# Where weights and activations stand in SBUF: one 64-byte offset moved from the weights to the activations

## The chip, the core and the metric

One Trainium2 chip, of which the kernel uses one core (8 are there). The metric is the device time of one execution in microseconds; what is compared is the median of several executions.

## What is computed

The reference runs two networks one after the other on 256 tokens of width 1,024, all in 32-bit floats. The first has two layers, each made of a gated feed-forward (2,816 hidden), a token-mixing part with three branches (RWKV-7, gated linear attention, gated delta rule), a second feed-forward and a projection with a gate. The second has one layer of attention over the tokens and 256 context tokens, a feed-forward over both streams, one HGRN2 layer and a last feed-forward. Cut to the pieces that hold nearly all the weights:

```python
def _swiglu(x, w1, w3, w2):
    return (jax.nn.silu(x @ w1) * (x @ w3)) @ w2

def token_mixing(x, w_in, ...):
    h = (x @ w_in).astype(jnp.float32)
    h_rw, h_gla, h_gdn, h_gate = _split(h, GROUP_SPLITS)
    ...
    proj = jnp.einsum('btnc,ncd->btnd', branches, w_branch)
    merged = jnp.sum(gates * proj, axis=2)
    return merged.astype(x.dtype) @ w_o
```

## The kernel before, in words

All large products are made in a split form: an operand is held as `hi`, rounded to the matmul's own 32-bit type, and `lo`, the rest, and a product is three matmuls, hi x hi, lo x hi and hi x lo. Weights come in units of 512 KB (128 partitions x 1,024 numbers). `unit` (line 70) calls `split` (line 74): SyncE's queue loads the unit into a buffer `wr`, ScalarE copies it into `wh` (line 81), VectorE subtracts into `wl` (line 82). There are four buffers each of `wr` and `wh` and three of `wl`; a unit takes the next of each in turn, so the same pair of `wh` and `wl` comes back every twelve units. Activations lie in SBUF as `xh` and `xl`, made once per stage.

Two kinds of stage use the units. In a feature-major stage (`fm`, lines 105 to 112) a block of 128 x 128 weights is the stationary operand and 256 columns of `xh` or `xl` stream past it; 24 matmuls (8 blocks, 3 products) fill one PSUM tile. The feed-forward `ffn2` calls it for two units and each stream in turn: unit A with the first stream, unit B with the first, then A and B with the second where there is one. Here the third product of the first pair of units is made in a pass of its own (line 112). In a token-major stage (`tm2`, lines 181 to 183) a block of `xh` or `xl` is stationary and 512 columns of weights stream past (256 at a stage's end). TensorE's program is in this order, and every matmul is preceded by the load of its own stationary operand.

The five feed-forward stages with one stream begin at 8.6, 629, 863, 1,497 and 2,632 us of the profiled execution (each 1,056 feature-major matmuls and then the token-major ones on the hidden values `hh` and `hl`), the one with two streams at 1,963 us (2,112). Between them lie token mixing (15 + 12 + 4 single units, cut up by the branches' own work, twice), attention, and HGRN2's gates (24 units).

What this change is about is where those tiles lie in a partition. A tile pool is placed behind the pool before it, in the order in which they are opened, and takes its tiles times its buffers. In bytes, before the change:

| tile | first buffer | next buffers |
|---|---|---|
| `wr` | 22,176 | 4,096 apart |
| `wh` | 38,560 | 4,224 apart (4) |
| `wl` | 55,456 | 4,224 apart (3) |
| `xh`, `xl` of the first stream | 68,128 and 76,320 | one each |
| `xh`, `xl` of the second stream | 109,216 and 117,408 | one each |
| `hh` of feed-forwards 1 and 3, of 2, of 4 | 109,120, 127,552, 156,320 | |
| `hh` of the second network | 129,696 (second stream 174,752) | |
| `bh` (branches) | 160,320 | |

A buffer of `wh` or `wl` has 32 numbers (128 bytes) more than a unit, and the unit lies in it at an offset `at` that depends on the use: 16 numbers (64 bytes) in feature-major stages (`FM_AT`), 8 numbers (32 bytes) for `bh` and for the hidden values of the first network (`HID_AT`), 0 for all else. Blocks within a unit and within an activation are 512 or 1,024 bytes apart, so they do not change an address modulo 256.

Of the kernel before, what the change touches and what calls it, by code (L numbers as in the profile page):

```python
# [10 lines left out]
F32 = mybir.dt.float32  # L11
F32R = mybir.dt.float32r
# [5 lines left out]
P = 128  # L18
# [4 lines left out]
KF = 22  # L23
# [6 lines left out]
PIECES = (slice(0, 256), slice(256, 1024))  # L30


ROOM, FM_AT, HID_AT = 32, 16, 8


class Core:


# [14 lines left out]
    def open(self, es):  # L53
        tc = self.tc
        E = es.enter_context
        self.const = E(tc.tile_pool(name="const", bufs=1))
        self.wr = E(tc.tile_pool(name="wr", bufs=WR))
        self.wh = E(tc.tile_pool(name="wh", bufs=4))
        self.wl = E(tc.tile_pool(name="wl", bufs=3))
        self.xp = E(tc.tile_pool(name="xp", bufs=1))  # L60
        self.sm = E(tc.tile_pool(name="sm", bufs=4))
        self.fr = None
        self.mhalf = self.const.tile([P, 16], F32, name="mhalf")
        self.nc.gpsimd.memset(self.mhalf, -0.5)
        self.fc = E(tc.tile_pool(name="fc", bufs=1))
        self.mx = None
        self.dr = E(tc.tile_pool(name="dr", bufs=1, space=bass.MemoryType.DRAM))

    def unit(self, src, at=0):
        self.tick()
        return self.split(src, at)

    def split(self, src, at):
        nc = self.nc
        hi = self.wh.tile([P, 1024 + ROOM], F32R, tag="wh", name=self.nm("wh"))[:, at:at + 1024]
        lo = self.wl.tile([P, 1024 + ROOM], F32R, tag="wl", name=self.nm("wl"))[:, at:at + 1024]
        raw = self.wr.tile([P, 1024], F32, tag="wr", name=self.nm("wr"))
        nc.sync.dma_start(raw, src)  # L80
        on_act = nc.scalar.copy(hi, raw)  # L81
        on_dve = nc.vector.tensor_tensor(lo, raw, hi.bitcast(F32), ALU.subtract)  # L82
        if self.queue:
            for op, first in zip((on_act, on_dve), self.queue.pop(0)):
                self.behind(op, first)
        return hi, lo
# [48 lines left out]
    def ffn2(self, up, down, xs, scale, sink, aside={}):  # L135


        nc = self.nc
        with self.tc.tile_pool(name=self.nm("hp"), bufs=1, reuse_waits="tile") as hp:
            hs = []  # L140
            for i in range(len(xs)):
                hs.append((hp.tile([P, KF, T], F32R, tag=f"hh{i}", name=self.nm("hh")),
                           hp.tile([P, KF, T], F32R, tag=f"hl{i}", name=self.nm("hl"))))
            for m in range(KF):
                if m == 3:
                    self.load_later()
                if m in aside:
                    aside[m]()
                w = [self.unit(up[2 * m], FM_AT), self.unit(up[2 * m + 1], FM_AT)]
                for (xh, xl), (hh, hl) in zip(xs, hs):  # L150
                    pa, pv = self.acc(), self.acc()
                    self.fm([pa[:, :T], pv[:, :T]], w, xh, xl, late=m == 0)
                    th = hp.tile([P, T], F32, tag="th", bufs=3, name=self.nm("th"))
                    nc.scalar.activation(th, pa[:, :T], AF.Tanh, scale=0.5)  # L154
                    g = hp.tile([P, T], F32, tag="g", bufs=3, name=self.nm("g"))
                    nc.vector.scalar_tensor_tensor(g, th, 1.0, pa[:, :T], ALU.add, ALU.mult)
                    nc.vector.scalar_tensor_tensor(g, g, 0.5 * scale, pv[:, :T], ALU.mult, ALU.mult)  # L157
                    nc.scalar.copy(hh[:, m], g)  # L158
                    nc.vector.tensor_tensor(hl[:, m], g, hh[:, m].bitcast(F32), ALU.subtract)
            self.spot("down")  # L160
            self.tm2(down, 0, 2, hs, KF, sink, cut=True, at=0 if self.fr is None else HID_AT)

    def tm(self, src, b0, nblk, xh, xl, nk, sink, last=6, cut=False, at=0):
        self.tm2(src, b0, nblk, [(xh, xl)], nk, lambda n, i, t, ps, *c: sink(n, t, ps, *c), last, cut=cut, at=at)

    def tm2(self, src, b0, nblk, xs, nk, sink, last=6, lead=0, cut=False, at=0):

        nc = self.nc  # L170
        w = {}

        def mm(z, k, b, first, end):
            u = b // 2
            if u not in w:
                w[u] = self.unit(src[u], at)
            o, i, t, c = z
            h, l = (x[:, (b % 2) * 512 + c.start:(b % 2) * 512 + c.stop] for x in w[u])
            s = slice(t * P, t * P + P)
            xh, xl = xs[i]  # L180
            nc.tensor.matmul(o, xh[:, k, s], h, start=first, stop=False)  # L181
            nc.tensor.matmul(o, xh[:, k, s], l, start=False, stop=False)  # L182
            nc.tensor.matmul(o, xl[:, k, s], h, start=False, stop=end)  # L183

        self.load_later()
        for n in range(nblk):
            it = [(self.acc(), i, t, slice(0, 512)) for i in range(len(xs)) for t in range(2)]
            if cut and n == nblk - 1:
                o, i, t, _ = it.pop()
                it += [(o[:, :256], i, t, slice(0, 256)), (self.spare()[:, :256], i, t, slice(256, 512))]  # L190
            ahead = lead if n == 0 else 0
            tail = 0 if n < nblk - 1 else min(nk - ahead, last if len(xs) == 1 else last // 2)
            seq = [(k, z) for i in (1, 0) for k in range(ahead) for z in it if z[1] == i]
            seq += [(k, z) for k in range(ahead, nk - tail) for z in it]
            for k, z in seq:
                mm(z, k, b0 + n * nk + k, k == 0, k == nk - 1)
            for z in it:
                for k in range(nk - tail, nk):
                    mm(z, k, b0 + n * nk + k, k == 0, k == nk - 1)
                o, i, t, c = z  # L200
                sink(n, i, t, o, *((c,) if cut else ()))
# [884 lines left out]
class Block(Mix):  # L1086
# [15 lines left out]
    def proj(self, l, n, o):  # L1102

        nc = self.nc
        first = not self.merged
        bh = self.t([P, 4, T], "bh", F32R, pool=self.late)
        bl = self.t([P, 4, T], "bl", F32R, pool=self.late)
        self.to_fm(lambda t: o[:, t], bh, bl, nk=4)

        def sink(half, t, ps):  # L1110
            g = self.gt[n, half]
            nc.vector.scalar_tensor_tensor(g[:, t], g[:, t], 1.0, ps, ALU.add, ALU.mult)
            if first:
                self.merged[half] = g
            else:
                m = self.merged[half]
                nc.gpsimd.tensor_tensor(m[:, t], m[:, t], g[:, t], ALU.add)
        self.tm(self.a["wbr"][l, n], 0, 2, bh, bl, 4, sink, at=HID_AT)

    def rw_tile(self, i, ps, st={}):  # L1120
        nc = self.nc
# [21 lines left out]

    def fm_tile(self, i):
        p = self.acc()[:, :T]
        self.fm([p], [self.unit(self.wfm[i], FM_AT)], self.xh, self.xl)
        return p

    def token_mix(self, l, pool, ln):
# [121 lines left out]
    def first(self, es, ep, stop=None):  # L1271
        nc, tc, a = self.nc, self.tc, self.a
# [6 lines left out]

        def last_pool():  # L1280
            self.xq = es.enter_context(tc.tile_pool(name="xq", bufs=1, reuse_waits="tile"))
            self.xq.tile([P, 24], F32, name="fillq")
            return self.xq
        self.consts()
        self.x_load(pool())
# [46 lines left out]
class Second(Block):  # L1332
# [371 lines left out]
    def hgrn(self, h, st, xs):  # L1704
        nc, tc, a = self.nc, self.tc, self.a
        V = nc.vector
        with tc.tile_pool(name="hg", bufs=1, reuse_waits="tile") as p:
# [9 lines left out]
            m = tl([P, KD], "lm")  # L1717
# [17 lines left out]
            xh, xl = (self.xp.tile([P, KD, T], F32R, tag=f"x{c}0", name=self.nm("xo")) for c in "hl")  # L1735
# [5 lines left out]
            def gates(j):  # L1741
# [1 line left out]

                z = tl([P, 4, T], "z", bufs=2)
                for d in range(2):
                    w = self.unit(a["whfm"][3 * j + d], FM_AT)
                    ps = self.acc()
                    for i in range(2):
                        self.fm([ps[:, i * T:i * T + T]], [w], *xs[i])
                    nc.scalar.activation(z[:, d:4:2], ps.rearrange("p (i t) -> p i t", i=2), AF.Tanh, scale=0.5)  # L1750
                pq = self.acc()[:, :T]
                self.fm([pq], [self.unit(a["whfm"][3 * j + 2], FM_AT)], *xs[0])
# [5 lines left out]
                c, cx = tl([P, 4 * W], "c", bufs=2), tl([P, 2, W], "cx", bufs=2)  # L1758
# [134 lines left out]
            last = self.fetches([tl([P, 2, D], k) for k in ("qx", "kx", "v0", "v1")])  # L1893
# [204 lines left out]
```

## Time and profile before

| | us |
|---|---|
| runs of the kernel before | 2,810.91, 2,817.24, 2,833.98 |
| their median | 2,817.24 |
| the profiled execution, its own time | 2,826.01 |
| its span, first to last instruction | 2,824.2 |
| busy in the span: TensorE, VectorE, ScalarE, GpSimd | 2,723.2, 1,891.3, 1,299.3, 201.6 |

Every number from the trace belongs to the one profiled execution. The mean granted TensorE clock over the span is 0.983 of full speed. Busy time of TensorE counts a matmul from its issue to its modelled end, and matmuls overlap in the pipeline, so the mean of one matmul is longer than the time from its start to the next one's.

### The profile page before, as it was taken

To read this page: it belongs to the slowest core of one execution; us is meant where nothing else is said; L and a number is where in the kernel's file an instruction comes from. 1 tells how busy PE (TensorE), PEld (TensorE's weight loads), DVE (VectorE), ACT (ScalarE), POOL (GpSimd) and SP (SyncE) were. 2 spreads that over 40 slices of the span, in tenths; PEclk is the share of its full clock that TensorE was granted. 3 is DMA by queue.
4 is the path that set the end of the run, shared out by engine and by line. 5 is a ranking of instruction groups with operands and counts; after the bars stand their busy time and mean duration, and the time that the engine had idled before them with its cause. 6 is when DMAs were issued, how large, how long until landed. Compare 5 with 4: busy or idle time off the path is not lost.

```text
span 2824.2 us, 47580 instructions
## 1 busy us (share of the span) xinstructions
PE 2723.2 (96%) x18676; PEld 2403.6 (85%) x18676; DVE 1891.3 (67%) x3852; ACT 1299.3 (46%) x2040; POOL 201.6 (7%) x332
## 2 busy tenths in 40 slices
PE   9999999999999999999999998999999999999998
PEld 8978877669978978887778986798999888898897
DVE  6658885876557658876777756776444327799765
ACT  5536543535444536533444533564333225565553
POOL 0000211020000000211010001200000001000000
PEclk9999999999999999999999999999999999999999
DMA  7664333466666655323366556202332333214664
GB/s 257 195 207 162 113 123 111 143 235 194 195 225 205 194 181 181 120 95 117 120 219 233 187 172 226 83 10 89 105 98 90 127 102 110 75 57 145 196 194 152
DMA packets 117008, 426.63 MB, mean 151 GB/s; under 512 B 13600, under 2 KB 14112, under 8 KB 115760
## 3 DMA queue, kind: packets, MB, share of 16 engines
q1 hardware_dynamic: 115168, 419.01, 44.7%
q0 software_dynamic: 1472, 4.51, 0.5%
q8 instruction: 147, 2.41, 0.4%
q14 instruction: 77, 0.63, 0.1%
q10 hardware_dynamic: 144, 0.07, 0.0%
HBM read 420.36 MB, written 3.18 MB: 150 GB/s over the span
## 4 chain that ended last, share of the span: by engine, by line
PE 82%; DVE 11%; ACT 3%; DMA 2%; issue 2%; POOL 0%; DVEq 0%; POOLq 0%; SPq 0%; ACTq 0%
PE ps L105 12%; PE ps L106 12%; PE ps L108 12%; PE ps L182 10%; PE ps L181 10%; PE ps L183 10%; DVE wl L82 2%; PE pc L490 2%; PE pc L1653 1%; PE pc L1399 1%; PE pt L246 1%; PE pt L1637 1%; ACT wh L81 1%; PE pt L1840 1%; PE pc L661 1%
## 5 line engine op out<-in xcount | busy, mean ns | idle before, releaser
L82 DVE TENSOR_TENSOR wl<-wr,wh 128x1024 fp32r<-128x1024 f32 x658 | 813.1, 1238 | 524.0 <-issue 184.3
L81 ACT CAST wh<-wr 128x1024 fp32r<-128x1024 f32 x658 | 687.9, 1048 | 632.0 <-PE ps L183 294.2
L105 PE MATMUL ps<-xh,wh 128*128 128x256 f32 x3280 | 924.1, 283 | 11.7 <-ACT xh L250 5.9
L106 PE MATMUL ps<-xh,wl 128*128 128x256 f32 x3280 | 918.3, 281 | 3.3 <-DVE wl L82 3.3
L108 PE MATMUL ps<-xl,wh 128*128 128x256 f32 x3168 | 885.4, 280 | 0.1
L105 PEld LDWEIGHTS ps<-xh,wh 128*128 128x128 f32 x3280 | 624.4, 190 | 23.7 <-ACT xh L250 7.1
L106 PEld LDWEIGHTS ps<-xh,wl 128*128 128x128 f32 x3280 | 623.1, 190 | 9.6 <-DVE wl L82 4.4
L108 PEld LDWEIGHTS ps<-xl,wh 128*128 128x128 f32 x3168 | 598.5, 189 | 5.2 <-issue 4.1
L181 PE MATMUL ps<-wh,xh 128*128 128x512 f32 (+1 forms) x624 | 246.7, 398 | 5.2 <-ACT wh L81 3.0
L182 PE MATMUL ps<-wl,xh 128*128 128x512 f32 (+1 forms) x624 | 248.2, 398 | 0.8 <-DVE wl L82 0.8
L183 PE MATMUL ps<-wh,xl 128*128 128x512 f32 (+1 forms) x624 | 245.6, 395 | 0.0
L181 PE MATMUL ps<-wh,hh 128*128 128x512 f32 (+1 forms) x616 | 227.7, 370 | 0.1
L183 PE MATMUL ps<-wh,hl 128*128 128x512 f32 (+1 forms) x616 | 227.2, 369 | 0.0
L182 PE MATMUL ps<-wl,hh 128*128 128x512 f32 (+1 forms) x616 | 226.9, 368 | 0.0
L181 PEld LDWEIGHTS ps<-wh,xh 128*128 128x128 f32 x624 | 118.4, 190 | 36.6 <-ACT wh L81 3.5
L182 PEld LDWEIGHTS ps<-wl,xh 128*128 128x128 f32 x624 | 119.6, 192 | 26.1 <-DVE wl L82 2.1
L183 PEld LDWEIGHTS ps<-wh,xl 128*128 128x128 f32 x624 | 119.1, 191 | 23.8 <-issue 0.7
L181 PEld LDWEIGHTS ps<-wh,hh 128*128 128x128 f32 x616 | 115.7, 188 | 21.6 <-DVE g L157 0.5
L183 PEld LDWEIGHTS ps<-wh,hl 128*128 128x128 f32 x616 | 115.6, 188 | 21.1
L182 PEld LDWEIGHTS ps<-wl,hh 128*128 128x128 f32 x616 | 115.8, 188 | 20.7
L154 ACT ACTIVATE th<-ps 128x256 f32<-128x256 f32 x154 | 59.2, 385 | 151.9 <-PE ps L108 141.3
L158 ACT CAST hh<-g 128x256 fp32r<-128x256 f32 x154 | 62.6, 406 | 114.9 <-DVE g L157 114.8
(566 smaller groups left out, 3714.7 us busy)
## 6 DMA issues: line engine op xcount, KB each, us to landing
wr<-in_up SPq DMA_DIRECT2D x264, 512.0 KB, 4.2
wr<-in_down SPq DMA_DIRECT2D x132, 512.0 KB, 4.2
wr<-in_wtm SPq DMA_DIRECT2D x72, 512.0 KB, 3.3
wr<-in_wfm SPq DMA_DIRECT2D x62, 512.0 KB, 3.5
fr<-in_ada SPq DMA_DIRECT2D x23, 1024.0 KB, 5.8
wr<-in_ada SPq DMA_DIRECT2D x38, 512.0 KB, 4.3
wr<-in_wbr SPq DMA_DIRECT2D x24, 512.0 KB, 4.0
wr<-in_whfm SPq DMA_DIRECT2D x24, 512.0 KB, 3.3
```

The costliest lines, as they stand in the source:

```text
L81: on_act = nc.scalar.copy(hi, raw)
L82: on_dve = nc.vector.tensor_tensor(lo, raw, hi.bitcast(F32), ALU.subtract)
L105: nc.tensor.matmul(o, hi[:, w], xh[:, k], start=k == 0, stop=False)
L106: nc.tensor.matmul(o, lo[:, w], xh[:, k], start=False, stop=False)
L108: nc.tensor.matmul(o, hi[:, w], xl[:, k], start=False, stop=k == nk - 1)
L154: nc.scalar.activation(th, pa[:, :T], AF.Tanh, scale=0.5)
L158: nc.scalar.copy(hh[:, m], g)
L181: nc.tensor.matmul(o, xh[:, k, s], h, start=first, stop=False)
L182: nc.tensor.matmul(o, xh[:, k, s], l, start=False, stop=False)
L183: nc.tensor.matmul(o, xl[:, k, s], h, start=False, stop=end)
L246: nc.tensor.transpose(pt[:, j, t * P:t * P + P], self.cols(src(t), t, k + j), self.ident)
L490: nc.tensor.matmul(ps[:, 64 * u:64 * u + 64], lhs[:, u], rhs[:, u], start=True, stop=True)
```

## The change

The spare room in the weights' buffers goes, and with it the offsets of units: every unit starts at its buffer's edge and the buffers lie 4,096 bytes apart. Instead three unused tiles stand ahead of the activations: 64 bytes (`fillx`) ahead of `xh` and `xl` of the first stream, 32 bytes (`fillf`) in the pool behind, which moves all later pools, and in the last pool, which holds the second stream, 64 bytes in place of 96 (`fillq`). No instruction is added, taken away or reordered. The added line `raw = lo.bitcast(F32)` has no effect, as `raw` is set anew in the next line.

```diff
-ROOM, FM_AT, HID_AT = 32, 16, 8
...
         self.xp = E(tc.tile_pool(name="xp", bufs=1))
+        self.xp.tile([P, 16], F32, name="fillx")
...
         self.fc = E(tc.tile_pool(name="fc", bufs=1))
+        self.fc.tile([P, 8], F32, name="fillf")
...
-        hi = self.wh.tile([P, 1024 + ROOM], F32R, tag="wh", name=self.nm("wh"))[:, at:at + 1024]
-        lo = self.wl.tile([P, 1024 + ROOM], F32R, tag="wl", name=self.nm("wl"))[:, at:at + 1024]
+        hi = self.wh.tile([P, 1024], F32R, tag="wh", name=self.nm("wh"))
+        lo = self.wl.tile([P, 1024], F32R, tag="wl", name=self.nm("wl"))
+        raw = lo.bitcast(F32)
         raw = self.wr.tile([P, 1024], F32, tag="wr", name=self.nm("wr"))
...
-                w = [self.unit(up[2 * m], FM_AT), self.unit(up[2 * m + 1], FM_AT)]
+                w = [self.unit(up[2 * m]), self.unit(up[2 * m + 1])]
...
-            self.tm2(down, 0, 2, hs, KF, sink, cut=True, at=0 if self.fr is None else HID_AT)
+            self.tm2(down, 0, 2, hs, KF, sink, cut=True)
...
-            self.xq.tile([P, 24], F32, name="fillq")
+            self.xq.tile([P, 16], F32, name="fillq")
```

The rest of the diff takes `at` out of `unit`, `split`, `tm`, `tm2` and of their calls for the branches, the token mixing and the gates.

## Rows read from the trace of the kernel before

**Rows 1.** The page's head, busy time by engine, and the chain by engine.
```profile
span 2824.2 us, 47580 instructions
...
PE 2723.2 (96%) x18676; PEld 2403.6 (85%) x18676; DVE 1891.3 (67%) x3852; ACT 1299.3 (46%) x2040; POOL 201.6 (7%) x332
...
PE 82%; DVE 11%; ACT 3%; DMA 2%; issue 2%; POOL 0%; DVEq 0%; POOLq 0%; SPq 0%; ACTq 0%
```

**Rows 2.** The page's groups: count, busy us, mean ns, idle before.
```profile
L82 DVE TENSOR_TENSOR wl<-wr,wh 128x1024 fp32r<-128x1024 f32 x658 | 813.1, 1238 | 524.0 <-issue 184.3
```

**Rows 3.** Windows: us, busy PE, PEld, DVE, ACT, POOL (instructions), clock, DMA, GB/s.
```profile
20.00:130.00 110.00, 110.00 (x973) 110.00 (x972) 72.16 (x103) 56.79 (x84) 0.00 (x0) 1.00 0.66 212
...
1510.00:1620.00 110.00, 110.00 (x967) 110.00 (x967) 75.75 (x116) 58.83 (x87) 0.00 (x0) 1.00 0.57 190
...
1970.00:2210.00 240.00, 239.74 (x2060) 239.20 (x2059) 109.03 (x190) 81.07 (x138) 0.00 (x0) 1.00 0.30 97
```

**Rows 4.** Windows cut at the starts of groups of 24, two-stream feed-forward.
```profile
2051.76:2054.59 2.83, 2.83 (x26) 2.83 (x25) 0.85 (x2) 0.41 (x1) 0.00 (x0) 1.00 0.00 0
2054.59:2057.44 2.85, 2.85 (x26) 2.85 (x25) 1.56 (x2) 1.32 (x2) 0.00 (x0) 1.00 0.11 20
...
2065.82:2068.54 2.72, 2.72 (x27) 2.72 (x25) 1.55 (x2) 1.32 (x2) 0.00 (x0) 1.00 0.17 26
...
2085.20:2088.04 2.84, 2.84 (x26) 2.84 (x25) 0.84 (x2) 0.41 (x1) 0.00 (x0) 1.00 0.00 0
2088.06:2090.90 2.84, 2.84 (x26) 2.84 (x25) 1.56 (x2) 1.32 (x2) 0.00 (x0) 1.00 0.20 42
```

**Rows 5.** Windows of two groups of 24 in the last feed-forward.
```profile
2643.68:2646.51 2.83, 2.83 (x27) 2.83 (x25) 2.21 (x4) 1.62 (x4) 0.00 (x0) 1.00 0.64 217
2649.34:2652.06 2.72, 2.72 (x26) 2.72 (x26) 1.56 (x2) 1.32 (x2) 0.00 (x0) 1.00 0.54 176
```

**Rows 6.** Windows inside feature-major groups that follow a pause of TensorE.
```profile
205.55:207.67 2.12, 2.12 (x20) 2.12 (x19) 1.25 (x3) 1.53 (x2) 0.00 (x0) 1.00 1.04 425
1081.06:1083.66 2.60, 2.60 (x25) 2.60 (x24) 2.60 (x12) 1.93 (x3) 0.11 (x2) 1.00 0.00 0
2504.50:2506.86 2.36, 2.36 (x22) 2.36 (x21) 2.36 (x9) 1.73 (x3) 0.00 (x0) 1.00 0.00 0
```

**Rows 7.** Groups by shape, whole span: the first product of feature-major stages.
```profile
L105 PE MATMUL ps<-xh,wh 128*128 128x256 f32 x3280 | 924.1, 283 | 11.7 <-ACT xh L250 5.9 <-ACT wh L81 3.5 <-ACT xh L255 1.9
```

**Rows 8.** Groups by shape, 756 to 810 us: token-major, 512 and 256 columns.
```profile
L183 PE MATMUL ps<-wh,hl 128*128 128x512 f32 x62 | 24.4, 393 | 0.0
...
L181 PE MATMUL pc<-wh,hh 128*128 128x256 f32 x16 | 4.5, 281 | 0.0
```

**Rows 9.** Groups by shape, 30 to 130 us: feature-major, one stream.
```profile
L105 PE MATMUL ps<-xh,wh 128*128 128x256 f32 x295 | 81.4, 276 | 0.0
```

**Rows 10.** Groups by shape, whole span: one of three token-major products, 512 columns.
```profile
L182 PE MATMUL ps<-wl,xh 128*128 128x512 f32 x584 | 237.1, 406 | 0.8 <-DVE wl L82 0.8
...
L182 PE MATMUL ps<-wl,hh 128*128 128x512 f32 x484 | 190.0, 393 | 0.0
...
L182 PE MATMUL ps<-wl,xc 128*128 128x512 f32 x48 | 19.5, 407 | 2.3 <-DVE wl L82 2.3
...
L182 PE MATMUL ps<-wl,xo 128*128 128x512 f32 x24 | 9.7, 405 | 0.0
```

**Rows 11.** Window of 14 token-major matmuls of 512 columns, last feed-forward.
```profile
2783.18:2786.36 3.18, 3.18 (x16) 2.63 (x15) 2.11 (x3) 1.51 (x2) 0.00 (x0) 1.00 0.67 215
```

**Rows 12.** Windows of token-major stages: hidden values of feed-forwards 2, 4 and last.
```profile
756.00:810.00 54.00, 54.00 (x282) 45.97 (x281) 25.48 (x25) 19.94 (x19) 0.00 (x0) 1.00 0.59 193
1626.00:1682.00 56.00, 56.00 (x289) 47.37 (x288) 26.54 (x28) 20.38 (x20) 0.00 (x0) 1.00 0.58 188
2757.00:2812.00 55.00, 55.00 (x287) 47.01 (x286) 28.26 (x25) 20.70 (x23) 3.18 (x3) 1.00 0.50 163
```

More of the change, by code (lines that the diff above doesn't have):

```diff
@@ L65, in open, with unit, split @@
         self.fc = E(tc.tile_pool(name="fc", bufs=1))
+        self.fc.tile([P, 8], F32, name="fillf")
         self.mx = None
         self.dr = E(tc.tile_pool(name="dr", bufs=1, space=bass.MemoryType.DRAM))
-    def unit(self, src, at=0):
+    def unit(self, src):
         self.tick()
-        return self.split(src, at)
-    def split(self, src, at):
+        return self.split(src)
+    def split(self, src):
         nc = self.nc
-        hi = self.wh.tile([P, 1024 + ROOM], F32R, tag="wh", name=self.nm("wh"))[:, at:at + 1024]
-        lo = self.wl.tile([P, 1024 + ROOM], F32R, tag="wl", name=self.nm("wl"))[:, at:at + 1024]
+        hi = self.wh.tile([P, 1024], F32R, tag="wh", name=self.nm("wh"))
+        lo = self.wl.tile([P, 1024], F32R, tag="wl", name=self.nm("wl"))
+        raw = lo.bitcast(F32)
         raw = self.wr.tile([P, 1024], F32, tag="wr", name=self.nm("wr"))
@@ L160, in ffn2, with tm, tm2 @@
             self.spot("down")
-            self.tm2(down, 0, 2, hs, KF, sink, cut=True, at=0 if self.fr is None else HID_AT)
-    def tm(self, src, b0, nblk, xh, xl, nk, sink, last=6, cut=False, at=0):
-        self.tm2(src, b0, nblk, [(xh, xl)], nk, lambda n, i, t, ps, *c: sink(n, t, ps, *c), last, cut=cut, at=at)
-    def tm2(self, src, b0, nblk, xs, nk, sink, last=6, lead=0, cut=False, at=0):
+            self.tm2(down, 0, 2, hs, KF, sink, cut=True)
+    def tm(self, src, b0, nblk, xh, xl, nk, sink, last=6, cut=False):
+        self.tm2(src, b0, nblk, [(xh, xl)], nk, lambda n, i, t, ps, *c: sink(n, t, ps, *c), last, cut=cut)
+    def tm2(self, src, b0, nblk, xs, nk, sink, last=6, lead=0, cut=False):
         nc = self.nc
@@ L175, in mm @@
             if u not in w:
-                w[u] = self.unit(src[u], at)
+                w[u] = self.unit(src[u])
             o, i, t, c = z
@@ L1117, in sink @@
                 nc.gpsimd.tensor_tensor(m[:, t], m[:, t], g[:, t], ALU.add)
-        self.tm(self.a["wbr"][l, n], 0, 2, bh, bl, 4, sink, at=HID_AT)
+        self.tm(self.a["wbr"][l, n], 0, 2, bh, bl, 4, sink)
     def rw_tile(self, i, ps, st={}):
@@ L1145, in fm_tile @@
         p = self.acc()[:, :T]
-        self.fm([p], [self.unit(self.wfm[i], FM_AT)], self.xh, self.xl)
+        self.fm([p], [self.unit(self.wfm[i])], self.xh, self.xl)
         return p
@@ L1745, in gates @@
                 for d in range(2):
-                    w = self.unit(a["whfm"][3 * j + d], FM_AT)
+                    w = self.unit(a["whfm"][3 * j + d])
                     ps = self.acc()
@@ L1751, in gates @@
                 pq = self.acc()[:, :T]
-                self.fm([pq], [self.unit(a["whfm"][3 * j + 2], FM_AT)], *xs[0])
+                self.fm([pq], [self.unit(a["whfm"][3 * j + 2])], *xs[0])
                 q = tl([P, T], "hq", bufs=2)
```

## The prediction

> **What bounds the kernel now.** First the head of the page [rows 1]: TensorE (PE) is busy 96% of a 2,824.2 us span, VectorE 67%, ScalarE 46%, and the chain that ended last is PE for 82%. Of the two lines that prepare each unit of weights, the costlier one comes to 813.1 us on VectorE [rows 2], so that engine is not the bound. The change adds, removes and reorders no instruction: it only moves tiles in SBUF. So the question is whether a matmul takes a different time when its operands lie elsewhere, and the second view for that is the busy time by stretch. In the five feature-major stages with one stream, PE is busy all 110 us of a 110 us window and starts 967 to 973 matmuls in it [rows 3]: 110.00/973 = 113.05 ns from start to start. In the feature-major stage with two streams the same instruction takes 240.00/2060 = 116.5 ns [rows 3], with the granted clock at 1.00 (2.4 GHz) in all of them and with PE busy throughout. So the pace differs where nothing waits. PE has no slack in these windows, so a nanosecond per matmul goes to the span one to one.
>
> Cut at single groups of 24 matmuls (one half of a unit pair, one stream), the two-stream stage shows just two paces [rows 4]: a group takes 2.72 us (113.3 ns each) or 2.83 to 2.85 us (118 to 119 ns). (A window's count also takes in the two or three matmuls that straddle its ends.) The pattern comes back 33.44 us later: the groups at 2051.76 and 2054.59 are long, and so are those at 2085.20 and 2088.06 [rows 4]. In that time the stage goes through twelve units, which is the least number after which the four hi and the three lo buffers meet again. I read this as a rhythm of the pair "matmul streams its moving operand, the next weight load reads beside it", set by the addresses. I call the two the short pitch (113.1 ns) and the long pitch (117.9 ns: 2.83 us/24 [rows 5]); 4.85 ns lie between them.
>
> With the addresses of the kernel section, the distance from moving operand to next weights, modulo 256, is 64 or 192 in every feature-major matmul, alternating with the buffer (4,224 is 128 more than 4,096 and so moves the distance by 128). What decides the pitch in the groups I went through: after a pause of PE it is drawn anew; without a pause a short pitch stays short while the stream stays; a change between the streams (41,088 bytes apart, 128 modulo 256) turns short into long; and the long pitch is left in units where hi stands at 64 and lo at 192. An instance is the last feature-major stage: it starts long, the group at 2643.68 (hi and lo both at 192) is long, the next one (64 and 192) leaves that pitch, and from 2649.34 it is short [rows 5]. In groups of the first stream alone with hi and lo at the same distance I found none that left the long pitch inside.
>
> **The change part by part.** After it, hi buffers lie at 38,560 + 4,096j and lo at 54,944 + 4,096j, xh of the first stream at 67,296, of the second at 108,384. So the distance is 192 for the first stream and 64 for the second in every unit, for hi and lo alike. What this does:
>
> (a) Feature-major, one stream: 5 x 1,056 matmuls. The units at (64, 192), which lead out of the long pitch now, are gone. A stage that starts long then stays long: 1,056 x 4.85 ns = 5.1 us. How often does one start long? Of thirteen groups that follow a pause with hi and lo both at 192, ten are long; the rows show the first and the last of the ten, 18 matmuls in 2.12 us and 20 in 2.36, and one of the three short ones, 23 in 2.60 [rows 6]. 10/13 x 5 x 5.1 = +19.7 us. Bounds: 0 (all start short) and +25.6.
>
> (b) Two streams: 2,112 matmuls. Each change of stream turns the pitch, so half of the groups are long: (113.05 + 117.9)/2 = 115.5 against 116.5 now, -2.2 us. Bounds: all short -7.3, all long +3.
>
> (c) The feature-major units inside token mixing and the gates (there are three matmuls for each of the 3,280 of [rows 7], 9,840; less the above, 2,448). They are cut up by other work, so they start anew often, now and later: 0, and 5 us either way if half of them change their pitch.
>
> (d) Token-major, 512 columns. A mean of 393 ns [rows 8] is, by the 163 ns that a short feature-major matmul lasts beyond its pitch (276 [rows 9] - 113), 230 ns from start to start. Now the distance is a multiple of 128 in these, apart from the fourth hidden stage. After the change it is 64 or 192 for all on xh, xc, xo and on the last hidden stages: by the counts of [rows 10] 3 x 584 + 3 x 48 + 3 x 24, and of the 3 x 484 on hh all but the 3 x 198 of the first three hidden stages, together 2,826. The first three hidden stages and bh keep a multiple of 128, since the 32 bytes of fillf are there. No row shows 512 columns at a distance of 64. Nearest on the good side: 14 in a row at one constant distance took 3.18 us, 227 ns each [rows 11], so -3 ns, as after the change each distance is constant. Further off, if both halves of the 512 columns lost the 4.85 ns between the two, -9.7 ns or -27 us. On the bad side: the fourth hidden stage, now at 96 or 224, takes 56.00/289 = 193.8 ns over its mix of shapes against 54.00/282 = 191.5 and 55.00/287 = 191.6 [rows 12], some +2.5 ns, +7 us. I take -2 ns, between the constant run and no change: -5.7 us.
>
> (e) Token-major, 256 columns, some 640 moved: 281 ns [rows 8] means the long pitch. At the new distance half may be short: 640 x -2.4 = -1.5 us, between -3 and 0.
>
> (f) Casts, transposes, DMAs and 32-bit matmuls: same instructions, same sizes. VectorE is busy 72.16 of 110 us in a feature-major window [rows 3] and 25.48 of 54 in a token-major one [rows 12]; they hide there, and if PE needs 2% less time they hide still. 0, or 2 us either way for the 32 bytes by which pools above the last one move against earlier ones, which may join or part two tiles that share an edge.
>
> At (a) a rule of the Trainium skill would have it otherwise. The row is that the same instruction takes 113 or 118 ns at an unchanged clock [rows 5]. "TensorE: Matmul & The Clock Gate", section "Step-by-step: what each phase is for", says that PE reads the moving operand and the weights through two independent ports, so that a weight load takes nothing from the running matmul. By that, no placement would matter and the sum would be 0; the two paces of one stage speak against it.
>
> **Sum.** +19.7 - 2.2 + 0 - 5.7 - 1.5 = +10.3 us. The profiled execution took 2,826.0 us (span 2,824.2 and 1.8 around it), 8.8 above the median 2,817.2. So 2,836 for such an execution and 2,827 for the median.
>
> **Rivals.** *The long pitch takes all, and the new distance is bad for token-major.* It decides if every start falls into the long pitch: (a) +25.6, (b) +3, (c) +5, (d) at its bad bound +7: +40, 2,857. For it: ten of thirteen starts, and no way out. Against it: starts are drawn several times at the head of a stage, and three of thirteen are short.
> *The short pitch takes all.* With equal buffers, what is short remains short, as in [rows 3] now; (a) 0, (b) -7.3, (c) -5, (d) -9.9 (227 ns) or -27, (e) -3: 2,792, or 2,775 at the far end. For it: 64 is the one distance at which the trace shows the short pitch. Against it: the starts.
> *Placement does nothing lasting*, the pitches being drawn as often as now, by the two-port rule or because other pauses decide them: 2,817. It would also come out so if (a) and (d) just cancel, which the forecast is not far from.
>
> **How the numbers follow.** The forecast with its near neighbours (three to five stages long, token-major between -3 and 0 ns) 0.50: 2,811 to 2,838. Nothing lasting 0.20: 2,817. All long 0.17: 2,838 to 2,857. All short 0.13: 2,775 to 2,800. About 1% (28 us) is what a measurement of this kernel can tell from no change: its three runs spread from 2,810.9 to 2,834.0. Slower by over 1% (over 2,845): all-long cases with the bad bound and the upper edge of the forecast, 0.18. Faster by over 1% (under 2,789): 0.11, most of the all-short case. Within: 0.71. The range takes in the forecast, the near part of both outer cases and the spread of the runs: 2,790 to 2,852.
>
> **What would show it.** In the changed trace the window 20 to 130 us should hold about 933 matmuls (117.9 ns) where a stage is long from end to end, 973 where it is short, and no stage should change its pitch in mid-course without a pause. The two-stream stage should alternate group pairs at 2.83 and 2.72 us with the stream, without the 33.44 us pattern. The by-shape mean of the 512-column matmuls on xh in an undisturbed window should go from 393 to about 391 ns, while those of the first three hidden stages stay. If the feature-major stages are short throughout, step (a) is wrong; if the 512-column mean falls below 387 or rises above 396 ns, step (d) is; if the subtraction on VectorE changes from 1,238 ns [rows 2], (f) is. The prediction is wrong altogether if a stage shows pauses of PE that are not there now.

## The result, and the profile after

The changed kernel takes 2,843.52 us (median of ten runs) against 2,821.16 (ten runs of the kernel before on the same chips): ratio 1.0081, 95% interval 1.0062 to 1.0100. It is 22.4 us slower, 0.8%. The forecast was 2,827, with a range of 2,790 to 2,852; the time lies in the range, 16.5 us above the point.

The head of the page after, the busy time by engine and the chain by engine, against [rows 1]: TensorE's busy time goes up by 22.3 us, VectorE's by 0.1, and the chain is TensorE's as before.

```profile
span 2841.5 us, 47580 instructions
...
PE 2745.5 (97%) x18676; PEld 2422.3 (85%) x18676; DVE 1891.4 (67%) x3852; ACT 1301.1 (46%) x2040; POOL 202.7 (7%) x332
...
PE 83%; DVE 11%; ACT 3%; issue 2%; DMA 1%; POOL 0%; DVEq 0%; POOLq 0%; ACTq 0%; SPq 0%
```

The groups by line, after (count, busy us, mean ns, idle before): the subtraction that was 1,238 ns [rows 2] still is, and the first product of the feature-major stages, 924.1 us in [rows 7], is 4.1 us dearer.

```profile
L104 PE MATMUL ps<-xh,wh 128*128 128x256 f32 x3280 | 928.2, 284 | 9.9 <-ACT xh L249 4.5 <-ACT wh L80 3.1 <-ACT xh L254 2.0
...
L81 DVE TENSOR_TENSOR wl<-wr,wh 128x1024 fp32r<-128x1024 f32 x658 | 812.9, 1238 | 545.2 <-issue 197.4 <-PE ps L181 146.0 <-PE ps L105 84.4
```

Windows of the changed kernel, columns as in [rows 3]: the five one-stream feature-major stages, the two-stream one, four of its groups of 24 (two of the second stream, then two of the first), and 120 token-major matmuls of 512 columns in a row, from start to start, in the hidden stages of feed-forwards 1, 2 and last.

```profile
20.00:130.00 110.00, 110.00 (x937) 110.00 (x936) 69.51 (x100) 54.47 (x79) 0.00 (x0) 1.00 0.64 207
640.00:750.00 110.00, 110.00 (x936) 110.00 (x936) 70.45 (x100) 55.88 (x81) 0.00 (x0) 1.00 0.58 187
880.00:990.00 110.00, 110.00 (x935) 110.00 (x934) 70.54 (x100) 55.87 (x81) 0.00 (x0) 1.00 0.59 187
1510.00:1620.00 110.00, 110.00 (x925) 108.14 (x925) 74.81 (x116) 58.38 (x89) 2.34 (x4) 0.99 0.59 189
2650.00:2760.00 110.00, 109.99 (x931) 109.56 (x931) 71.43 (x103) 56.34 (x82) 0.51 (x1) 1.00 0.57 187
1980.00:2220.00 240.00, 239.63 (x2033) 239.09 (x2032) 108.18 (x188) 80.80 (x137) 0.00 (x0) 1.00 0.29 95
...
2051.52:2054.34 2.82, 2.82 (x27) 2.82 (x26) 0.85 (x2) 0.41 (x1) 0.00 (x0) 1.00 0.00 0
2054.34:2057.16 2.82, 2.82 (x27) 2.82 (x26) 1.56 (x2) 1.32 (x2) 0.00 (x0) 1.00 0.20 51
2057.16:2060.00 2.84, 2.84 (x27) 2.84 (x26) 1.98 (x3) 1.46 (x2) 0.00 (x0) 1.00 0.58 176
2060.00:2062.80 2.80, 2.80 (x27) 2.80 (x26) 0.42 (x1) 0.38 (x1) 0.00 (x0) 1.00 0.40 151
...
137.41:165.41 28.00, 28.00 (x122) 22.52 (x121) 13.12 (x13) 10.98 (x12) 0.00 (x0) 1.00 0.58 189
762.82:790.70 27.88, 27.88 (x121) 22.61 (x120) 13.12 (x13) 10.98 (x12) 0.00 (x0) 1.00 0.59 191
2773.63:2801.09 27.46, 27.46 (x121) 22.54 (x120) 14.94 (x13) 10.96 (x12) 2.41 (x1) 1.00 0.65 214
```

TensorE is busy throughout, at the full clock (0.99 in one window), and starts 937 matmuls in the window that held 973: the long pitch, from end to end in four of the five one-stream stages; in the other, the fourth feed-forward, four groups between two pauses ran short. In the two-stream stage both streams are long (2.80 to 2.84 us a group), where before 2.72 and 2.83 both occurred [rows 4]. Token-major matmuls of 512 columns are 28.00/120 = 233.3 ns apart where the distance is a constant 128, and 228.8 where it is a constant 192.

To get the whole sum I took, from the trace's list of matmuls, the time from each start to the next, left out what is over 150 ns (256 columns) or 300 ns (512) in either kernel, which are pauses, and compared the kernels stage by stage. After minus before: feature-major +26.4 us (one stream +21.0, two streams +3.1, token mixing and gates +2.2), token-major +1.8 (512 columns +2.5, 256 columns -0.7); together +28.1. Pauses that these stages share took 5.0 us less, and everything else 5.8 less, which is no more than two executions of one kernel differ by: the profiled one of before was 4.9 us over the median of its ten.

### The profile page after: what moved, and what is told of

Read it like the earlier page. It is cut to its first block, busy times and chain, and to the rows that moved or that the text cites. A ratio compares the mean times of both kernels' runs of the same rounds, so it can differ in the third digit from the quotient of the medians.

```text
span 2841.5 us, 47580 instructions
## 1 busy us (share of the span) xinstructions
PE 2745.5 (97%) x18676; PEld 2422.3 (85%) x18676; DVE 1891.4 (67%) x3852; ACT 1301.1 (46%) x2040; POOL 202.7 (7%) x332
## 4 chain that ended last, share of the span: by engine, by line
PE 83%; DVE 11%; ACT 3%; issue 2%; DMA 1%; POOL 0%; DVEq 0%; POOLq 0%; ACTq 0%; SPq 0%
PE ps L104 13%; PE ps L105 13%; PE ps L107 12%; PE ps L181 10%; PE ps L180 9%; PE ps L182 9%; DVE wl L81 2%; PE pc L489 2%; PE pc L1398 1%; PE pc L1652 1%; PE pt L245 1%; ACT wh L80 1%; PE pt L1636 1%; PE pt L1839 1%; PE pc L660 1%
## 5 line engine op out<-in xcount | busy, mean ns | idle before, releaser
L81 DVE TENSOR_TENSOR wl<-wr,wh 128x1024 fp32r<-128x1024 f32 x658 | 812.9, 1238 | 545.2 <-issue 197.4
L182 PEld LDWEIGHTS ps<-wh,xl 128*128 128x128 f32 x624 | 118.8, 190 | 24.5 <-issue 0.7
```

## The experiments

Theory after the result: the two pitches (113 and 118 ns) are a state that TensorE keeps from matmul to matmul; a unit with hi at 64 and lo at 192 leads out of the long one; with hi and lo at one distance there is no way out. Rivals: A, the 64 bytes under the activations cost by themselves; B, buffers congruent modulo 4,096 (their starts a multiple of it apart) cost; C, the loss is in the token-major stages. In what follows, "hi 64, lo 192" gives the distance from moving operand to weights modulo 256 in feature-major stages.

**1. The buffers 4,224 bytes apart again**

```diff
-        hi = self.wh.tile([P, 1024], F32R, tag="wh", name=self.nm("wh"))
-        lo = self.wl.tile([P, 1024], F32R, tag="wl", name=self.nm("wl"))
+        hi = self.wh.tile([P, 1024 + 32], F32R, tag="wh", name=self.nm("wh"))[:, :1024]
+        lo = self.wl.tile([P, 1024 + 32], F32R, tag="wl", name=self.nm("wl"))[:, :1024]
```

> The changed kernel with its weights' buffers 4,224 bytes apart again (units at the edge, activations still 64 bytes past the weights' phase), so that the feature-major distance alternates between 64 and 192 from buffer to buffer as before the change, and the 512-column token-major distance alternates between 64 and 192 too, which no kernel had. Theory (the long pitch stays because hi and lo of every unit stand at one distance; a unit with hi at 64 and lo at 192 leads out of it): the one-stream windows of 110 us hold 965 to 973 matmuls again, the two-stream window of 240 us 2,050 to 2,065, and the time comes back to that of the kernel before, ratio 0.997 to 1.003. Rival A (the 64 bytes under the activations cost by themselves): 936 per window and ratio 1.007 to 1.010. Rival B (buffers congruent modulo 4,096 cost): as the theory. Rival C (the loss is in the token-major stages): pitch short, ratio still 1.005 or more.

Measured: 2,816.36 us, ratio 0.9984 (0.9971 to 0.9997). Windows of it: one stream, two streams, the last feed-forward.

```profile
20.00:130.00 110.00, 110.00 (x973) 110.00 (x973) 72.06 (x104) 56.40 (x84) 0.00 (x0) 1.00 0.61 211
...
1960.00:2180.00 220.00, 219.81 (x1892) 219.62 (x1892) 97.55 (x163) 71.69 (x122) 0.00 (x0) 1.00 0.29 99
2630.00:2730.00 100.00, 100.00 (x885) 100.00 (x884) 65.22 (x93) 51.16 (x73) 0.00 (x0) 1.00 0.60 199
```

973 again, and 1,892 in 220 us are 2,064 in 240. The activations are where the change put them, so A falls; C falls too as it was stated, since the ratio would have stayed at 1.005. What is left is that all units stand alike, or that the buffers are congruent (B).

**2. One distance, buffers not congruent**

```diff
+        i, self.ui = self.ui, self.ui + 1
+        h0 = 32 * ((0, 3, 2, 1)[i % 4] % 2 if i < 591 else (0, 1, 3, 2)[(i - 591) % 4] % 2)
+        l0 = 32 * ((0, 2, 1)[i % 3] % 2 if i < 590 else (i - 590) % 3 % 2)
...
-        hi = self.wh.tile([P, 1024 + 32], F32R, tag="wh", name=self.nm("wh"))[:, :1024]
+        hi = self.wh.tile([P, 1024 + 32], F32R, tag="wh", name=self.nm("wh"))[:, h0:h0 + 1024]
```

(and `lo` with `l0`; the lists are the order in which the buffers come round).

> The first kernel of this call with every second buffer's unit 128 bytes further in, so that all units stand at one phase modulo 256 but no two buffers are congruent modulo 2,048 (starts 38,560, 42,912, 47,008, 51,360): feature-major distance 64 for hi and lo alike in the first stream and 192 in the second (after the change it is 192 and 64). Theory: one distance for hi and lo keeps the long pitch whichever it is: 930 to 940 per 110 us and 2,030 to 2,040 per 240 us, feature-major +26 us; token-major on xh now at a constant 192, 229 ns in place of 231 (-4 us); ratio 1.005 to 1.009. Rival B (only buffers congruent modulo 4,096 cost): 967 to 973 per window, ratio 0.997 to 1.002. Rival D (192 is the costly distance, 64 is not): 973 per window in the one-stream stages, ratio below 1.0.

Measured: 2,822.21 us, ratio 1.0015 (0.9996 to 1.0033). Its windows, the five one-stream stages in order and the two-stream one ahead of the last:

```profile
20.00:130.00 110.00, 110.00 (x936) 110.00 (x935) 69.26 (x100) 54.51 (x79) 0.00 (x0) 1.00 0.61 208
640.00:740.00 100.00, 100.00 (x885) 100.00 (x883) 66.26 (x94) 52.11 (x75) 0.00 (x0) 1.00 0.58 195
880.00:980.00 100.00, 100.00 (x884) 100.00 (x884) 64.81 (x92) 51.30 (x74) 0.00 (x0) 1.00 0.59 197
1500.00:1600.00 100.00, 100.00 (x867) 100.00 (x867) 69.42 (x107) 53.94 (x80) 0.00 (x0) 1.00 0.54 186
1970.00:2190.00 220.00, 220.00 (x1870) 220.00 (x1869) 95.99 (x162) 70.93 (x119) 0.00 (x0) 1.00 0.29 98
2640.00:2740.00 100.00, 100.00 (x885) 100.00 (x884) 66.42 (x94) 52.50 (x76) 0.00 (x0) 1.00 0.59 198
```

A miss in the time, which lies where rival B had put it, and half a miss in the windows. The first stage is long from end to end and the two-stream stage too (1,870 in 220 us: 117.6 ns), but three stages are short from end to end (885 in 100 us: 113.0 ns) and one changes at pauses. So one distance doesn't mean the long pitch; it means that a stage keeps, from pause to pause, the pitch with which it starts. Of the starts after a pause that show a clear pitch 13 of 32 were short, where the changed kernel has 2 of 35 (such counts move by one to three with what is called clear). That left open whether the distance (64 or 192) or the congruence sets the odds; 6 and 7 answer it.

**3 and 4. hi at 64 and lo at 192 in every unit**

3 puts 128 bytes between the hi and the lo buffers of the changed kernel; 4 adds 128 more ahead of the second stream.

```diff
+        self.fw = E(tc.tile_pool(name="fw", bufs=1))
+        self.fw.tile([P, 32], F32, name="fillw")
         self.wl = E(tc.tile_pool(name="wl", bufs=3))
...
-            self.xq.tile([P, 16], F32, name="fillq")
+            self.xq.tile([P, 48], F32, name="fillq")
```

> The changed kernel with 128 unused bytes between the hi and the lo buffers and nothing else: hi stands at 64 and lo at 192 in every unit of the first stream, at 192 and 64 in the second; buffers still 4,096 apart, units at the edge. Theory: each unit leads out of the long pitch, so the five one-stream stages hold 970 to 975 matmuls per 110 us from their first group on; in the two-stream stage the second stream is drawn into the long pitch or not, 2,033 to 2,120 per 240 us; feature-major 8 to 12 us below the kernel before, ratio 0.994 to 0.999. Rivals A and B (shift of the activations; buffers congruent modulo 4,096): 936 per window, ratio 1.006 to 1.010.

> The third kernel of this call with 128 bytes more ahead of the second stream, so that both streams stand at the same phase and hi is at 64 and lo at 192 for both. Theory: the two-stream stage is short as well, 2,110 to 2,120 matmuls per 240 us (6 us below the kernel before), the one-stream stages as in the third kernel; ratio 0.992 to 0.998. Rival E (a change of stream turns the pitch whatever the distances): the two-stream stage stays at 2,033 to 2,065 per 240 us. Rivals A and B: 936 per 110 us.

Measured: 3 takes 2,817.17 us, 0.9994 (0.9975 to 1.0012); 4 takes 2,809.88, 0.9977 (0.9961 to 0.9993), and a second time (10), beside 11 and 12, 2,811.29, 0.9971 (0.9956 to 0.9986):

> The kernel with both streams at 64 and 192 a second time, beside the two that follow on the same chip, to see whether what the token-major matmuls gain reaches the time. Expected: ratio 0.996 to 0.999 as before (0.9977).

Windows of 3: a one-stream stage, the two-stream stage, and four of its groups, first stream, second, second, first.

```profile
20.00:130.00 110.00, 110.00 (x973) 110.00 (x972) 71.89 (x103) 56.60 (x83) 0.00 (x0) 1.00 0.63 215
...
1980.00:2200.00 220.00, 219.79 (x1891) 219.43 (x1891) 99.04 (x168) 73.37 (x123) 0.00 (x0) 1.00 0.29 98
...
2054.20:2056.90 2.70, 2.70 (x26) 2.70 (x25) 0.42 (x1) 0.38 (x1) 0.00 (x0) 1.00 0.44 165
2056.90:2059.80 2.90, 2.90 (x27) 2.90 (x27) 0.84 (x2) 0.41 (x1) 0.00 (x0) 1.00 0.00 0
2059.80:2062.70 2.90, 2.90 (x27) 2.90 (x26) 1.56 (x2) 1.32 (x2) 0.00 (x0) 1.00 0.18 40
2062.70:2065.40 2.70, 2.70 (x26) 2.70 (x26) 1.98 (x3) 1.46 (x2) 0.00 (x0) 1.00 0.55 177
```

Windows of 4: the two-stream stage, and 120 token-major matmuls on the hidden values of feed-forwards 2 and last.

```profile
1960.00:2180.00 220.00, 219.85 (x1934) 219.29 (x1933) 102.90 (x178) 76.90 (x130) 0.00 (x0) 1.00 0.29 99
...
752.95:780.95 28.00, 28.00 (x122) 22.55 (x120) 13.13 (x13) 11.00 (x12) 0.00 (x0) 1.00 0.57 191
2739.48:2767.12 27.64, 27.64 (x122) 22.54 (x120) 14.95 (x13) 10.97 (x12) 2.40 (x1) 1.00 0.64 212
```

The buffers are 4,096 bytes apart, the units at their edges and the activations 64 bytes in, as in the changed kernel, and the one-stream stages are short: B falls, and A once more. In 3 the pitch follows the stream: all 42 groups of the second stream (hi 192, lo 64) are long, and every one of the 20 groups that come back from it to the first stream is short at once. So a mix of distances isn't enough: here a stream that begins at 64 and 192 is short, and one that begins at 192 and 64 is long. But 192 and 64 alone doesn't make the long pitch: in the kernel before, the group at 2065.82 us [rows 4] stands at 192 and 64 as well, in the second stream, and is short, because the unit ahead of it in that stream, at 64 and 192, had ended short. In 3 the long pitch comes in where the stream changes. In 4 all 42 groups of the second stream are short too, and the stage holds 1,934 in 220 us, 113.8 ns each, against 116.5 [rows 3]; rival E falls. That is where 4 gains over the kernel before: two streams -5.6 us, the gates of HGRN2 -2.6.

**6 and 7. One distance, the two crossings**

6 is the changed kernel with 192 bytes ahead of the activations in place of 64 (one distance of 64, buffers congruent); 7 is 2 the other way round (one distance of 192, not congruent).

```diff
-        self.xp.tile([P, 16], F32, name="fillx")
+        self.xp.tile([P, 48], F32, name="fillx")
```

```diff
-        h0 = 32 * ((0, 3, 2, 1)[i % 4] % 2 if i < 591 else (0, 1, 3, 2)[(i - 591) % 4] % 2)
-        l0 = 32 * ((0, 2, 1)[i % 3] % 2 if i < 590 else (i - 590) % 3 % 2)
+        h0 = 32 - 32 * ((0, 3, 2, 1)[i % 4] % 2 if i < 591 else (0, 1, 3, 2)[(i - 591) % 4] % 2)
+        l0 = 32 - 32 * ((0, 2, 1)[i % 3] % 2 if i < 590 else (i - 590) % 3 % 2)
```

> The changed kernel with 192 bytes in place of 64 ahead of the activations and nothing else: feature-major distance a constant 64 in the first stream (192 after the change), 192 in the second; buffers still 4,096 apart. Theory (at one distance a pitch stays as drawn, and at 64 a short one is drawn in 13 of 32 starts, as with the kernel at a constant 64 and buffers not congruent; at 192 in 2 of 35): one to four of the five one-stream stages long from end to end, no long stage turning short without a pause, two-stream stage long (2,030 to 2,040 per 240 us); ratio 0.999 to 1.006. Rival B (buffers congruent modulo 4,096 cost): all five at 936 per 110 us, feature-major +25 us, ratio 1.005 to 1.010.

> The kernel at a constant 64 with buffers not congruent, the other way round: a constant 192 in the first stream and 64 in the second, as after the change, but buffers not congruent modulo 2,048. Theory (at a constant 192 nearly every start is long): all five one-stream stages at 930 to 940 per 110 us, two-stream 2,030 to 2,040 per 240 us, feature-major +24 to +28 us and token-major +2, ratio 1.006 to 1.010, the changed kernel's own. Rival B (congruence is what made all five long): one to four stages short, ratio 0.999 to 1.005.

Measured: 6 takes 2,824.46 us, 1.0014 (1.0000 to 1.0029); 7 takes 2,843.38, 1.0093 (1.0075 to 1.0110). Windows of 6, the first three one-stream stages:

```profile
20.00:130.00 110.00, 110.00 (x973) 110.00 (x972) 72.12 (x104) 56.61 (x84) 0.00 (x0) 1.00 0.61 212
640.00:740.00 100.00, 100.00 (x852) 100.00 (x851) 62.26 (x89) 48.88 (x71) 0.00 (x0) 1.00 0.58 191
880.00:980.00 100.00, 100.00 (x885) 100.00 (x884) 65.27 (x92) 51.62 (x74) 0.00 (x0) 1.00 0.58 198
```

Windows of 7, the same stages:

```profile
20.00:130.00 110.00, 110.00 (x936) 110.00 (x935) 69.64 (x101) 54.53 (x82) 0.00 (x0) 1.00 0.61 207
640.00:740.00 100.00, 99.96 (x848) 99.88 (x848) 64.48 (x92) 51.39 (x76) 0.00 (x0) 1.00 0.56 185
880.00:980.00 100.00, 100.00 (x845) 100.00 (x844) 64.37 (x92) 51.27 (x75) 0.00 (x0) 0.99 0.56 186
```

At 64 with congruent buffers three stages are short, one is long and one changes at pauses, as in 2 (though which stages are long differs); at 192 without congruence all five are long, as in the changed kernel. So B has no part in it, and the odds of a start go with the distance: 14 of 29 clear starts short in 6, 4 of 35 in 7. In 7 both operands lie 128 bytes (modulo 256) from where the changed kernel has them, at the same distance, and the time is the same. 128 more unused bytes (6 against the changed kernel) take two thirds of the loss away; they move all later pools too, so a part of that, 5 us, is in token-major stages (the table below).

**8. One load in three at the other distance**

```diff
         xh = self.xp.tile([P, KD, T], F32R, tag="xh0", name=self.nm("xh"))
+        if not self.gap:
+            self.gap = self.xp.tile([P, 32], F32, name="fillz")
         xl = self.xp.tile([P, KD, T], F32R, tag="xl0", name=self.nm("xl"))
```

> The changed kernel with 128 unused bytes between xh and xl of the first stream: weights beside xh stay at 192 (hi and lo alike), and the third product's moving operand xl puts the next hi at 64, so one load in three stands at the other distance. Theory 1 (any mix of the two distances leads out of the long pitch): 970 to 975 per 110 us in the one-stream stages, ratio 0.996 to 1.002. Theory 2 (it takes hi at 64 beside xh and lo at 192): 930 to 940, ratio 1.005 to 1.010. The two-stream stage at 2,030 to 2,060 per 240 us by either.

Measured: 2,841.86 us, 1.0095 (1.0070 to 1.0120). Windows of the first two one-stream stages:

```profile
20.00:130.00 110.00, 110.00 (x936) 110.00 (x935) 69.63 (x101) 54.55 (x81) 0.00 (x0) 1.00 0.59 206
640.00:740.00 100.00, 100.00 (x856) 100.00 (x856) 64.43 (x91) 51.24 (x74) 0.00 (x0) 1.00 0.57 189
```

The load beside `xl` alone leads nowhere; the first stage is long. The second and third run in a third rhythm, 100.00/856 = 116.8 ns, with a gap of 112 or 113 ns at every ninth matmul among gaps of 114 to 121. Theory 2 holds for the time; the third rhythm shows that there are more than two paces.

**5, 11 and 12. Token-major at one distance**

From 4, the lo unit of token-major stages goes back 128 bytes (`odd` tells which of the three buffers it is, as in 2; the buffers of `lo` lie 4,224 bytes apart for it); 11 is 5 a second time, beside 4; 12 adds 64 bytes ahead of the hidden values of the last three feed-forwards.

```diff
-        lo = self.wl.tile([P, 1024], F32R, tag="wl", name=self.nm("wl"))
+        l0 = 32 * (1 - odd if fm else odd)
+        lo = self.wl.tile([P, 1024 + 32], F32R, tag="wl", name=self.nm("wl"))[:, l0:l0 + 1024]
...
+            self.nf += 1
+            if self.nf > 3:
+                hp.tile([P, 16], F32, tag="fillh", name=self.nm("fillh"))
```

> The kernel with hi at 64 and lo at 192 for both streams, and the lo unit of token-major stages put back 128 bytes, so that there hi and lo stand at one distance: 0 for the first network's hidden values and bh (there 0 and 128 before), 192 for xh, xc and the second network's hidden values (192 and 64 before). Feature-major is untouched. Theory (a 512-column matmul at a constant 0 takes 228 ns from start to start, at a constant 192 229 to 230, against 231 to 232 where the distance alternates): 2,800 of them by -1.5 to -4 ns, 6 to 9 us below the kernel with both streams at 64 and 192, ratio 0.992 to 0.996, and that kernel's feature-major windows (973 per 110 us) kept. Rival (the token-major distance only shows as noise of the profile): same time as that kernel, ratio 0.997 to 0.999.

> The kernel with token-major hi and lo at one distance a second time. The profile showed 8.6 us less for matmuls that follow each other without a gap than in the kernel with both streams at 64 and 192, the medians of the first time only 2.8 us less after allowing for the runs of before. Theory (the gain reaches the time, the first difference was drawn from runs that spread by 15 us): 5 to 9 us below the run beside it, ratio 0.993 to 0.996. Rival (it is eaten by waits for weights in the token-major stages, which are now reached sooner): within 3 us of it.

> The same with 64 bytes ahead of the hidden values of the last three feed-forwards, so that these too stand at a constant 0 in token-major stages (192 before): some 860 matmuls of 512 columns from 229.0 to 228.2 ns, -0.7 us, not to be told from the run beside it in time; in the profile their mean in an undisturbed window goes down by 1 ns or less.

Measured: 5 takes 2,807.08 us, 0.9966 (0.9951 to 0.9982), less of a gain than expected; the second time 2,802.81, 0.9938 (0.9916 to 0.9960), 8.5 us below 4 beside it (2,811.29); 12 takes 2,803.90, 0.9947 (0.9925 to 0.9969). Windows of 5 the second time, 120 matmuls on hidden values as above:

```profile
750.93:778.13 27.20, 27.20 (x121) 22.52 (x120) 13.11 (x13) 10.99 (x12) 0.00 (x0) 1.00 0.57 192
2734.95:2762.42 27.47, 27.47 (x122) 22.54 (x120) 14.75 (x13) 11.00 (x12) 2.40 (x1) 1.00 0.65 212
```

And of 12, the last feed-forward:

```profile
2739.11:2766.31 27.20, 27.20 (x121) 22.53 (x120) 14.60 (x13) 11.00 (x12) 2.40 (x1) 1.00 0.64 218
```

A constant 0 gives 27.20/120 = 226.7 ns, a constant 192 228.9, a constant 128 or 64 232.3 to 233.3, and before the change, with 0 and 128 in turn, it was 231.3. (These are windows without a pause; over whole stages a constant 0 gives 228.2 ns.) The first time, 5 gained only 0.6 us more than 4, each against the runs of before beside it (-9.5 and -8.9; the 2.8 us in the expectation of 11 is the plain difference of the two medians). The second time it was 8.5 us. By the table below the small difference of the first time goes with the granted clock: the gain reaches the time, and the rival of 11 falls. 12 shows its 2.2 ns in the window on the hidden values (0.7 to 1.1 ns over whole stages) and nothing in the time, since its 256-column matmuls lose more (+2.1 us) than the hidden ones of 512 columns gain in sum (-0.7): at 192 some ran 113.3 ns apart, at 0 118.6.

Over all runs the sum of these start-to-start times goes with the time (us, kernel minus kernel before; each median is set against that of the runs of before beside it):

| | feature-major | token-major | sum | median | at equal clock |
|---|---|---|---|---|---|
| the change | +26.4 | +1.8 | +28.1 | +22.4 | +25.6 |
| 1 | -1.3 | -0.3 | -1.6 | -2.4 | -1.2 |
| 2 | +9.1 | -3.3 | +5.8 | +3.4 | +6.5 |
| 3 | -2.8 | +0.6 | -2.2 | -1.6 | -0.8 |
| 4, and again | -10.2, -10.4 | -0.3, -0.1 | -10.5, -10.5 | -8.9, -6.6 | -7.0, -7.9 |
| 5, and again | -9.8, -9.9 | -8.9, -9.4 | -18.7, -19.3 | -9.5, -15.0 | -14.5, -15.7 |
| 6 | +8.9 | -3.4 | +5.5 | +7.8 | +5.5 |
| 7 | +26.3 | +2.2 | +28.5 | +26.8 | +25.9 |
| 8 | +26.3 | -1.1 | +25.3 | +25.2 | +24.5 |
| 12 | -10.2 | -7.7 | -17.9 | -13.9 | -14.0 |

The last column allows for TensorE's mean granted clock in each run. Over the 76 runs of the kernel before that stand beside the experiments (clock 0.977 to 0.987, time 2,811.4 to 2,834.7 us) the two go together with a correlation of -0.96, 2.1 us less for each 0.001 more; the column is the median distance of a kernel's runs from that line. It takes out most of the spread. The twelve first runs of 5 had 0.982 on average and those of before beside them 0.984, and at equal clock 5 is 7.5 us ahead of 4 the first time and 7.8 the second. In most rows it is 1 to 4 us smaller than the sum; where those go was not looked into.

## Why the prediction came out as it did

The frame held: what changed is the pitch of matmuls, TensorE had no slack where they follow each other, and no new wait came in. The terms:

- (a) right in mechanism, a little small in size: +21.0 us, expected +19.7 with +25.6 as bound. All five stages are long, not 10/13 of them; four cost 4.1 to 4.5 us, the fourth feed-forward 3.4, since four of its groups ran short after a pause at 1,567 us. The step that was mis-sized is the lottery: ten of thirteen was counted over hi and lo at 192 in a kernel that mixes its distances, and after the change 33 of 35 clear starts are long. That the units at 64 and 192 are the way out was read from single groups of before [rows 5]; 1, 3 and 4 show it.
- (b) wrong: +3.1 where -2.2 was expected, the value that the prediction gave as its bound. The failed sentence is "Each change of stream turns the pitch". The trace of before has 41 changes of stream between whole groups in that stage. The 27 that begin from the short pitch all start long (7 of them, into a unit at 64 and 192, end the group short). Of the 14 that begin from the long pitch 7 turn short inside the group, all between units with hi and lo both at 64, and 7 stay long, all between units at 192 and 64. So the turn to short was there, but not at every change, and I took it for a rule. The first row below is a long group of the first stream, the second the group of the second stream behind it, which turns short after five matmuls. After the change, from a constant 192 to a constant 64 and back, all 41 stay long; in 3 and 4 the pitch behind a change goes with the distances of the stream that begins. A rule that covers all of these cases is not known. (In HGRN2's gates, where the same unit goes on from one stream to the other, 8 of 10 such changes do turn long to short after the change, so one distance without a way out holds inside a stream and not at every change; why is not settled.)

```profile
2071.36:2074.20 2.84, 2.84 (x27) 2.84 (x26) 0.42 (x1) 0.38 (x1) 0.00 (x0) 1.00 0.44 163
2074.20:2076.94 2.74, 2.74 (x27) 2.74 (x25) 0.85 (x2) 0.41 (x1) 0.00 (x0) 1.00 0.00 0
```

- (c) +2.2 us, within its bounds of 5 either way.
- (d) wrong: +2.5 us where -5.7 was expected. "As after the change each distance is constant" is what failed: constant is not good by itself. A constant 64 (xh and xo of the first stream) costs 233.2 ns against 231.3, as the mean of those that follow each other. The 128 that the first three hidden stages now keep in every unit costs 232.3 to 233.3; the prediction had these stages and bh at no change, and they took 1.3 us more. Only the last hidden stages, at 192, gained (-1.6 us). The row of 227 ns [rows 11] was a true pace, that of a constant 0, which 5 then had; it was the wrong neighbour for 64. The by-shape mean that I named as a test was to fall from 393 to 391 on xh and to stay in the first three hidden stages. It rose in both: on xh by about 1 ns in a stretch of 88 matmuls without a pause (first row below before, second after; from start to start 20.13/87 = 231.4 ns and 20.30/87 = 233.3), and from 393 [rows 8] to 395 for the hidden values of feed-forward 2 (762 to 816 us, after). The bound of 396 ns that was to show (d) wrong was not passed, so it was set too wide.

```profile
407.72:427.85 20.13, 20.13 (x89) 16.34 (x87) 19.49 (x63) 9.91 (x12) 7.11 (x4) 1.00 0.59 182
411.84:432.14 20.30, 20.30 (x89) 16.27 (x88) 19.66 (x63) 9.93 (x12) 7.24 (x5) 1.00 0.58 181
...
L182 PE MATMUL ps<-wh,hl 128*128 128x512 f32 x61 | 24.1, 395 | 0.0
```

- (e) -0.7 where -1.5 was expected; (f) nothing, as expected.

The sum was +28.1 instead of +10.3, and the median rose by 22.4. Of the 17.8 us between the two sums, 13.5 come from (b) and (d), whose mechanisms were wrong, and both missed to the same side. The time lies above the forecast's own interval (2,811 to 2,838) and in that of the all-long case (2,838 to 2,857, chance 0.17). That it fell into the range is owed to the width of the range, which took in a part of that case, and not to the sum. Two slips of the working changed little: the 33.44 us of the two-stream pattern are six units and not twelve (each unit serves both streams, so twelve groups are six units, after which the distances repeat), and in the short-pitch rival 3 ns on 2,826 matmuls are -8.5 us, not -9.9. Of the rivals, "the long pitch takes all, and the new distance is bad for token-major" is the one that happened, with smaller terms ((c) +2.2, (d) +2.5) than its +40. "Placement does nothing lasting" falls with 6 against the changed kernel: 128 unused bytes more, the same instructions, and +7.8 us over the kernel before in place of +22.4. By the two-port rule of the Trainium skill ("TensorE: Matmul & The Clock Gate", "Step-by-step: what each phase is for"), as the prediction read it, these two would be the same; the measurement decides.

What stays open is what in the chip makes the state: the runs show distances that lead into it and out of it, not why. Nor does a run separate the next load's weights, which the prediction had in mind, from those that the matmul itself works with: inside a group of 24 the two give the same distances in every kernel here.

## What to carry to other kernels

Where TensorE is the bound and never waits, count the matmuls in equal windows; if the same instruction comes at two paces at one clock, cut the stage at groups and write the addresses of both operands, modulo 256, beside each. Placement is then a thing to tune, here for 0.3 to 0.8%, use by use: here hi at 64 and lo at 192 bytes past the moving activations, and both at one distance, 0 or 192, where the weights move, gave 0.9938 (0.9916 to 0.9960), and 0.9966 (0.9951 to 0.9982) the first time. That an arrangement is uniform does not make it good: in the one-stream stages a uniform one kept whatever pace the last pause left. And two kernels that differ by a few microseconds are compared at the same granted clock.

## What the runs showed of the hardware that was not expected

- A 256-column matmul on 32-bit operands takes 113 or 118 ns from start to start at the full clock. Which of the two goes with the byte distance between moving operand and weights, modulo 256, and with the pace before: the pace is kept over hundreds of matmuls (2: one stage all long, three all short with the same distances). At 64 and 192 all groups of the two-stream stage end short (before, 1, 3, 4); a stream that begins at 192 and 64 is long (3), while a single such unit met in the short pace stays short (before). At 64 throughout either pace occurs, at 192 throughout nearly always the long one.
- 512 columns, without a pause: 226.7 ns at a distance of 0, 228.9 at 192, 232.3 to 233.3 at 128 and 64, 231.3 where 0 and 128 take turns.
- Most of the spread between runs of one kernel goes with the mean granted clock: 2.1 us for each 0.001, over 76 runs of the kernel before.
- The spacing of buffers (4,096 against 4,224) and the place of the activations made no difference by themselves (1, 6, 7).
- With one load in three at another distance a third pace appeared, 116.8 ns (8).
